# Second feed-forward of a macaron layer: the rests of its weights made by a negating cast on ScalarE and an accumulating transfer of the raw weights

## The chip, the cores and the metric

The kernel runs on one core of a Trainium2 chip. The metric is device time in microseconds (us), the median of several executions. One further execution was taken by the hardware profiler; its page and its trace are what the sections below read. PE is TensorE, DVE VectorE, ACT ScalarE, POOL GpSimd, SP SyncE.

## The reference: what is computed

One decoder layer on 512 tokens of 1024 features, all in float32: a SwiGLU feed-forward, a token mixing with eight heads, and a second SwiGLU feed-forward. Each is wrapped in two RMS norms and modulated by a condition vector.

```python
y = rmsnorm(h, ffn1_pre_g) * (1.0 + sc1) + sh1
y = swiglu(y, ffn1_w_gate, ffn1_w_up, ffn1_w_down)       # (silu(y @ w_gate) * (y @ w_up)) @ w_down, width 2816
h = h + 0.5 * g1 * rmsnorm(y, ffn1_post_g)
y = rmsnorm(h, mix_pre_g) * (1.0 + sc2) + sh2
y = token_mix(y, ...)                                    # ends in merged @ w_out
h = h + g2 * rmsnorm(y, mix_post_g)
y = rmsnorm(h, ffn2_pre_g) * (1.0 + sc3) + sh3
y = swiglu(y, ffn2_w_gate, ffn2_w_up, ffn2_w_down)
h = h + 0.5 * g3 * rmsnorm(y, ffn2_post_g)
```

## The kernel before, in words

**Products in three parts.** PE multiplies in the type float32r, which keeps fewer bits than float32. Every operand w is therefore kept as two float32r tiles: hi, which is w cast to float32r, and lo, the rest w - hi. `mm3` (lines 98 to 101) adds three products into PSUM: hi·hi (line 99), left hi · right lo (line 100), left lo · right hi (line 101). The product lo·lo is left out.

**A unit of weights.** Weights come in units of 128 partitions x 1024 float32, 512 KB each. `unit` (lines 83 to 96) loads one into a raw tile on the SP queue (line 88), casts it to hi on ACT (line 94), and subtracts on DVE (line 95):

```python
        nc.scalar.copy(hi, raw)
        nc.vector.tensor_tensor(out=lo, in0=raw, in1=hi.bitcast(F32), op=ALU.subtract)
```

The pools `wraw` and `wsp` hold four raw tiles, four hi tiles and four lo tiles, so unit u can be cast only when PE is done with the hi tile of unit u - 4. Each unit feeds 24 matmuls of 512 columns.

**Names.** A unit's name tells its stage: `a_f_g` and `b_f_g` are gate (g = 0) and up (g = 1) weights of the first and second feed-forward, `da_half_u` and `db_half_u` their down weights, `dm_half_u` those of w_out at the end of the token mixing, `ft`, `vh` and `mv` the other weights of the mixing. The hi and lo tiles of unit `db_1_0` are `h_db_1_0` and `l_db_1_0`; the profile leaves buffer numbers out and shows `h_db` and `l_db`. PSUM tiles are `pub` (up products of the second feed-forward), `pdm` and `pdb` (down products of the mixing and of the second feed-forward).

**The down products** (`down`, lines 223 to 268) go in two halves of 512 output features, each with four accumulators, one for 128 tokens. `db` has 11 units in a half. Units 0 to 6 are used as they come, 24 matmuls each. The last four units are held and used together, token tile by token tile: for i in 0 to 3, for u in 7 to 10, 6 matmuls. So the four hi tiles come free only at the end of a half, 6 matmuls apart, and the first four units of the next half take their place. `dm` has 4 units in a half: its first half uses them as they come, its second half holds all four.

**Second feed-forward** (`ffn2`): the first three up tiles f = 0, 1, 2 are computed for the first 256 tokens, then for the other 256, while the mixing's last two token tiles are still being normalised and transposed (`pst`). Tile f = 2 is split into space in `hT` (`dst` is given), the other tiles into the pool. From f = 3 on `up_tile` takes whole tiles, and one gate load `ada` goes with each until they are used up.

**Order.** The program is written with tile pools; a scheduler puts the instructions of each engine in order and adds the waits. Each engine runs its instructions in that order. POOL's instructions late in the program are the powers -1/2 of the norms (`rpm` and `rs`, lines 277 and 162) and some elementwise steps of the mixing (lines 574 and 590).

Of the kernel before, what the change touches and what calls it, by code (L numbers as in the profile page):

```python
# [17 lines left out]
D = 1024  # L18
# [10 lines left out]
def layer_kernel(ctx: ExitStack, tc: tile.TileContext, x, c, cols, gate_b,  # L29
# [21 lines left out]

# [1 line left out]
    h = resid.tile([P, NT, D], F32, name="h")  # L53
# [13 lines left out]

    # silu of the condition, a copy on every partition
    sg = small.tile([P, T], F32, tag="x2", name="sg")[0:2, :]
# [8 lines left out]

    # 1 + bias of the scales
    bs1 = const.tile([P, 24], F32, name="bs1")  # L80
    nc.gpsimd.tensor_scalar(bs1, col[:, 24:48], 1.0, None, ALU.add)

    def unit(src, n, name, dst=None, park=None):
        if park is None:
            raw = wraw.tile([P, 1040], F32, tag="raw", name=f"r_{name}")[:, :n]
        else:
            raw = wsp.tile([P, 1040], F32, tag=park, name=f"r_{name}")[:, :n]
        nc.sync.dma_start(raw, src)
        if dst is None:
            hi = wsp.tile([P, 1040], F32R, tag="hi", name=f"h_{name}")[:, :n]  # L90
            lo = wsp.tile([P, 1040], F32R, tag="lo", name=f"l_{name}")[:, :n]
        else:
            hi, lo = dst
        nc.scalar.copy(hi, raw)  # L94
        nc.vector.tensor_tensor(out=lo, in0=raw, in1=hi.bitcast(F32), op=ALU.subtract)  # L95
        return hi, lo
# [5 lines left out]

# [1 line left out]
    modc = [const.tile([P, 3, KT], F32, name=f"modc{s}") for s in range(3)]  # L104

    def ada(s, kind, j):
        """128 of the scales (0), shifts (1) or gates (2) of sub-layer s, features on partitions"""
        raw = wraw.tile([P, 1040], F32, tag="raw", name=f"a_{s}_{kind}_{j}")[:, :D]
        pieces = 2 if s + j == 0 and kind < 2 else 1
        for q in range(pieces):  # L110
            sl = slice(q * D // pieces, (q + 1) * D // pieces)
            nc.sync.dma_start(raw[:, sl], ada_w[(s * 3 + kind) * KT + j, :, sl])
        init = bs1[:, s * KT + j:s * KT + j + 1] if kind == 0 else col[:, 24 * (kind + 1) + s * KT + j:][:, 0:1]
        v = modc[s][:, kind, j:j + 1]
        parts = 4
        w = D // parts
        acc = v if parts == 1 else small.tile([P, 4], F32, tag="part", name=f"part{s}_{kind}_{j}")
        for q in range(parts):
            sl = slice(q * w, (q + 1) * w)
            nc.vector.tensor_tensor_reduce(out=raw[:, sl], in0=raw[:, sl], in1=sc[:, sl], scale=1.0,  # L120
                                           scalar=init if q == 0 else 0.0, op0=ALU.mult, op1=ALU.add,
                                           accum_out=acc[:, q:q + 1])
        if parts > 1:
            nc.vector.tensor_reduce(out=v, in_=acc[:, :parts], axis=AX.X, op=ALU.add)
# [7 lines left out]
    def gate_rows(s):  # L132
        """gate times post-norm gain, a row on every partition; sqrt(D) goes with the root of a sum in post"""
        g = modc[s][:, 2, :]
        nc.vector.tensor_tensor(out=g, in0=g, in1=col[:, 152 + s * KT:152 + (s + 1) * KT], op=ALU.mult)
        nc.vector.tensor_scalar(g, g, (1.0 if s == 1 else 0.5) * float(D) ** 0.5, None, ALU.mult)
        gates[s] = dram.tile([1, D], F32, name=f"gd{s}")
        nc.sync.dma_start(gates[s].rearrange("o (j p) -> p (o j)", p=P), g)
# [11 lines left out]
    def normed(i, s, halves=False):  # L150
        """the norm of token tile i of h, before its gain: two halves of the features"""
        if halves:
            n = [small.tile([P, T], F32, tag="ysb", name=f"n{s}_{i}_{q}", bufs=4) for q in range(2)]
            t = junk
        else:
            t = tmp_tile(f"n{s}_{i}")
            n = [t[:, :T], t[:, T:]]
        ss = small.tile([P, 1], F32, tag="ss", name=f"ss{s}_{i}", bufs=6)
        nc.scalar.activation(t, h[:, i, :], AF.Square, accum_out=ss)
        r = small.tile([P, NT], F32, tag="rstd", name=f"rs{s}_{i}", bufs=6)[:, :1]  # L160
        nc.vector.tensor_scalar(r, ss, 1.0 / D, EPS, ALU.mult, ALU.add)
        nc.gpsimd.tensor_tensor(out=r, in0=r, in1=mhalf[:, :1], op=ALU.pow)
        if not halves:
            nc.vector.tensor_scalar(t, h[:, i, :], r, None, ALU.mult)
            return n
        for q in range(2):
            nc.scalar.activation(n[q], h[:, i, q * T:(q + 1) * T], AF.Copy, scale=r)
        return n
# [7 lines left out]
    def y_token_tile(s, i, y, n):  # L176
        """n, the norm of token tile i of h, modulated, split and with features on partitions"""
        ts_ = slice(i * P, (i + 1) * P)
# [22 lines left out]

# [1 line left out]
    def swiglu_evac(f, psg, psu, hT, tag):  # L203
# [19 lines left out]
    def down(wd, hT, tag, s, nxt, n=NF, order=lambda f: f, pump=None, drain=None, rest=()):  # L223
        """h += gate * rmsnorm(hT.T @ wd); then, a token tile at a time, nxt = (sub-layer, y), the input of the next
        sub-layer, or the output. Returns what is still to be issued for the last two token tiles."""
        t0, ss0, later = [], [], []
# [57 lines left out]

# [1 line left out]
    def ffn1():  # L286
# [82 lines left out]

# [1 line left out]
    def mix(y, later):  # L371
        with ExitStack() as mc:
# [19 lines left out]

            # lower bound of the forget gates: first row of a softmax over two
            l0, l1 = col[:, 136:140], col[:, 140:144]
# [15 lines left out]

            # dependent chains of small products, issued between the parts of the projections
            chains = [[], []]
# [19 lines left out]

            # values of both groups, tokens on partitions
            vh = mp.tile([P, NT, T], F32, name="vh")
# [25 lines left out]

            # gates of the matrix memory: heads on partitions, time along the free dimension
            rowb = x2("rowb")[:NH, :]
# [43 lines left out]
            def merge(c, o, gate):  # L506
                """o: [token in tile, tile, channel] of a head, normalised; gate: [channel, token]"""
                pt = tr_tile(f"pmt{c}")
                for i in range(NT):
                    nc.tensor.transpose(pt[:, i * P:(i + 1) * P], o[:, i * P:(i + 1) * P], ident)  # L510
                t = x2s(f"mt{c}")
                nc.vector.scalar_tensor_tensor(out=t, in0=pt, scalar=col[:, 144 + c:145 + c], in1=gate,
                                               op0=ALU.mult, op1=ALU.mult)
                nc.scalar.copy(mhi[:, c, :], t)
                nc.vector.tensor_tensor(out=mlo[:, c, :], in0=t, in1=mhi[:, c, :].bitcast(F32), op=ALU.subtract)

            def transposed(name, k):
                """the first three blocks of 128 of k [channel, token], tokens on partitions: in PSUM, and a tile for it"""
                ps = tr_tile(f"pkt{name}")
# [5 lines left out]
            def states(S, pv, decay):  # L525
                """S[j] = decay[j] S[j - 1] + pv[j]"""
                nc.scalar.copy(S[:, 0, :], pv[:, 0, :])
# [3 lines left out]

            # the gated recurrence: channels on partitions
            def hgrn_head(hd):
# [31 lines left out]
                def raise_level(b, t):  # L565
                    """queries and keys from blocks of b to blocks of 2 b; t: products of the gates of blocks of b"""
                    n2 = T // (2 * b)
# [30 lines left out]
                def state():  # L598
                    """the state after each of the first three blocks of 128"""
                    ps = mm_tile(f"pu{hd}")  # L600
# [32 lines left out]

            # the matrix memory: causal convolution along the free dimension, silu; quadratic form
            def mlstm_head(hd):
# [23 lines left out]
                def weights():  # L659
                    """exponentials, arguments at most 0: rows s of the diagonal blocks; the queries' and the keys'  # L660
                    weights against the maximum at a block's end; the states' decays"""
                    E = s["E"] = mp.tile([P, 7 * P + 8], F32, tag="E", name=f"E{hd}", bufs=2)
# [118 lines left out]

# [1 line left out]
    def ffn2(y, later):  # L783
# [108 lines left out]
```

## Time and profile before

| | |
|---|---|
| three executions | 1060.78 us median, 1059.91 to 1061.39 |
| the profiled execution, first to last instruction (its own time is not listed apart) | 1058.7 us |
| PE busy | 1037.4 us, 98% of the span, clock granted 0.999 of full |
| DVE busy | 602.5 us, 57% |
| ACT busy | 344.6 us, 33% |
| POOL busy | 70.4 us, 7% |
| DMA | 136.39 MB, 129 GB/s on average |

The span is read first, then each engine's share of it; a busy PE close to the span says that other engines matter only where they make PE wait. Matmuls overlap: the profile gives one of 512 columns about 390 ns, while the next starts some 230 ns after it. The median lies 2.1 us above the profiled span; that is work before the first and after the last instruction, and run to run variation.

### The profile page before, as it was taken

To read this page: it belongs to the slowest core of one execution; us is meant where nothing else is said; L and a number is where in the kernel's file an instruction comes from. 1 tells how busy PE (TensorE), PEld (TensorE's weight loads), DVE (VectorE), ACT (ScalarE), POOL (GpSimd) and SP (SyncE) were. 2 spreads that over 40 slices of the span, in tenths; PEclk is the share of its full clock that TensorE was granted. 3 is DMA by queue.
4 is the path that set the end of the run, shared out by engine and by line. 5 is a ranking of instruction groups with operands and counts; after the bars stand their busy time and mean duration, and the time that the engine had idled before them with its cause. 6 is when DMAs were issued, how large, how long until landed. Compare 5 with 4: busy or idle time off the path is not lost.

```text
span 1058.7 us, 13118 instructions
## 1 busy us (share of the span) xinstructions
PE 1037.4 (98%) x4988; PEld 855.8 (81%) x4988; DVE 602.5 (57%) x1426; ACT 344.6 (33%) x496; POOL 70.4 (7%) x104
## 2 busy tenths in 40 slices
PE   6999999999999999999999999999999999999997
PEld 4788888888888878978888888898888888888886
DVE  7985465566555275388879775775543434322323
ACT  5542233222212164444343323632322222211311
POOL 1000000000000020021223140100000000000000
PEclk9999999999999999999999999999999999999999
DMA  9864444444555413333223311144353222222212
GB/s 339 278 219 144 155 144 159 159 159 167 191 179 162 151 61 128 108 122 111 100 80 102 98 61 60 56 148 148 126 138 121 99 85 96 100 100 80 100 40 80
DMA packets 42938, 136.39 MB, mean 129 GB/s; under 512 B 7670, under 2 KB 8054, under 8 KB 42876
## 3 DMA queue, kind: packets, MB, share of 16 engines
q1 hardware_dynamic: 42588, 135.41, 37.9%
q8 instruction: 39, 0.64, 0.2%
q10 hardware_dynamic: 288, 0.16, 0.1%
q14 instruction: 23, 0.19, 0.1%
HBM read 133.43 MB, written 2.12 MB: 128 GB/s over the span
## 4 chain that ended last, share of the span: by engine, by line
PE 84%; DVE 9%; DMA 2%; issue 2%; POOL 1%; ACT 1%; SPq 0%; DVEq 0%; POOLq 0%; ACTq 0%
PE pub L100 7%; PE pub L99 7%; PE pub L101 7%; PE pua L100 7%; PE pua L99 7%; PE pua L101 7%; PE pdb L99 4%; PE pdb L101 4%; PE pdb L100 4%; PE pda L99 4%; PE pda L101 4%; PE pda L100 4%; PE pft L99 3%; PE pft L100 3%; PE pft L101 3%; PE pl L561 2%
## 5 line engine op out<-in xcount | busy, mean ns | idle before, releaser
L100 PE MATMUL pub<-ylo,h_b 128*128 128x512 f32 (+1 forms) x368 | 137.6, 374 | 0.0
L99 PE MATMUL pub<-yhi,h_b 128*128 128x512 f32 (+1 forms) x368 | 137.6, 374 | 0.0
L101 PE MATMUL pub<-yhi,l_b 128*128 128x512 f32 (+1 forms) x368 | 137.1, 373 | 0.0
L100 PE MATMUL pua<-ylo,h_a 128*128 128x512 f32 x304 | 119.6, 394 | 0.0
L99 PE MATMUL pua<-yhi,h_a 128*128 128x512 f32 x304 | 119.5, 393 | 0.0
L101 PE MATMUL pua<-yhi,l_a 128*128 128x512 f32 x304 | 119.3, 392 | 0.0
L94 ACT CAST h_b<-r_b 128x1024 fp32r<-128x1024 f32 x42 | 44.0, 1050 | 140.1 <-issue 103.6
L95 DVE TENSOR_TENSOR l_b<-r_b,h_b 128x1024 fp32r<-128x1024 f32 x42 | 51.3, 1224 | 61.6 <-ACT h_b L94 61.6
L120 DVE CUSTOM_DVE_ANT_0 a<-a,sc 128x256 f32<-128x256 f32 x216 | 82.5, 426 | 0.0
L94 ACT CAST h_a<-r_a 128x1024 fp32r<-128x1024 f32 x38 | 39.9, 1050 | 125.4 <-issue 78.9
L99 PEld LDWEIGHTS pub<-yhi,h_b 128*128 128x128 f32 x368 | 69.2, 188 | 13.2
L100 PEld LDWEIGHTS pub<-ylo,h_b 128*128 128x128 f32 x368 | 69.3, 188 | 13.0 <-DVE ylo L199 0.2
L101 PEld LDWEIGHTS pub<-yhi,l_b 128*128 128x128 f32 x368 | 69.2, 188 | 13.0
L99 PE MATMUL pft<-yhi,h_ft 128*128 128x512 f32 x192 | 79.1, 412 | 0.0
L100 PE MATMUL pft<-ylo,h_ft 128*128 128x512 f32 x192 | 75.6, 394 | 0.0
L101 PE MATMUL pft<-yhi,l_ft 128*128 128x512 f32 x192 | 75.6, 394 | 0.0
L99 PE MATMUL pda<-h_da,hThi 128*128 128x512 f32 x176 | 69.5, 395 | 0.0
L99 PE MATMUL pdb<-h_db,hThi 128*128 128x512 f32 x176 | 69.3, 394 | 0.0
L101 PE MATMUL pda<-h_da,hTlo 128*128 128x512 f32 x176 | 69.2, 393 | 0.0
L101 PE MATMUL pdb<-h_db,hTlo 128*128 128x512 f32 x176 | 69.2, 393 | 0.0
L100 PE MATMUL pdb<-l_db,hThi 128*128 128x512 f32 x176 | 69.0, 392 | 0.0
L100 PE MATMUL pda<-l_da,hThi 128*128 128x512 f32 x176 | 69.0, 392 | 0.0
(270 smaller groups left out, 1936.7 us busy)
## 6 DMA issues: line engine op xcount, KB each, us to landing
a<-in_ada_w_dram SPq DMA_DIRECT2D x70, 512.0 KB, 4.0
r_b<-in_wgu_dram SPq DMA_DIRECT2D x44, 512.0 KB, 3.5
r_a<-in_wgu_dram SPq DMA_DIRECT2D x38, 512.0 KB, 3.9
r_ft<-in_w_ft_dram SPq DMA_DIRECT2D x24, 512.0 KB, 3.2
r_da<-in_wd_dram SPq DMA_DIRECT2D x22, 512.0 KB, 3.2
r_db<-in_wd_dram SPq DMA_DIRECT2D x22, 512.0 KB, 3.5
r_dm<-in_w_out_dram SPq DMA_DIRECT2D x8, 512.0 KB, 4.8
r_s<-in_wgu_dram SPq DMA_DIRECT2D x12, 256.0 KB, 6.7
```

Source lines behind the costliest of these rows:

```text
L94: nc.scalar.copy(hi, raw)
L95: nc.vector.tensor_tensor(out=lo, in0=raw, in1=hi.bitcast(F32), op=ALU.subtract)
L99: nc.tensor.matmul(ps, lhs[0], rhs[0], start=start, stop=False)
L100: nc.tensor.matmul(ps, lhs[0], rhs[1], start=False, stop=False)
L101: nc.tensor.matmul(ps, lhs[1], rhs[0], start=False, stop=stop)
L120: nc.vector.tensor_tensor_reduce(out=raw[:, sl], in0=raw[:, sl], in1=sc[:, sl], scale=1.0, scalar=init if q == 0 else 0.0, op0=ALU.mult, o ...
L561: nc.tensor.matmul(pv[:, i, :], kk[:, sl], qq[:, sl], start=True, stop=True)
```

## The change

For units of the stages `b`, `db` and `dm` that are split into the pool, the subtraction on DVE is gone. In its place ACT casts once more, hi to lo with the scale -1, and POOL issues a transfer that reads the raw weights again from DRAM and adds them to lo. What is left in lo is w - hi as before. Two units of `b` (tile f = 2, with `dst` given) and the stages `a`, `da`, `ft`, `vh` and `mv` keep the subtraction. Other lines of the diff take comments away and move line numbers by 4 behind line 95.

```diff
@@ -92,7 +92,11 @@
         else:
             hi, lo = dst
         nc.scalar.copy(hi, raw)
-        nc.vector.tensor_tensor(out=lo, in0=raw, in1=hi.bitcast(F32), op=ALU.subtract)
+        if dst is None and name[0] in "bd" and name[:2] != "da":
+            nc.scalar.activation(lo, hi.bitcast(F32), AF.Copy, scale=-1.0)
+            nc.gpsimd.dma_start(lo, src, accum_op=ALU.add)
+        else:
+            nc.vector.tensor_tensor(out=lo, in0=raw, in1=hi.bitcast(F32), op=ALU.subtract)
         return hi, lo
```

72 units take the new path: 42 of `b`, 22 of `db`, 8 of `dm`.

Three places show how the scheduler answers. The first is ACT where the second feed-forward's weights are first cast, at the end of the mixing; before, with `yf`, `n` and `yhi` belonging to the norm of the mixing's token tiles:

```order
L94 CAST h_b_0_5573<-r_b_0_5571 128x1024
L190 ACTIVATE yf_1_0_5512<-pst_1_0_5507,modc_108 128x128 x2
L159 ACTIVATE n_2_5494,ss_2_5495<-h 128x1024
L190 ACTIVATE yf_1_0_5512<-pst_1_0_5507,modc_108 128x128 x2
L198 CAST yhi_5090<-yf_1_1_5524 128x4x128
L94 CAST h_b_1_5579<-r_b_1_5577 128x1024
L94 CAST h_b_0_5585<-r_b_0_5583 128x1024
```

With the change, at the same place (line 96 is the negating cast):

```order
L94 CAST h_b_0_5581<-r_b_0_5579 128x1024
L194 ACTIVATE yf_1_0_5520<-pst_1_0_5515,modc_108 128x128 x4
L163 ACTIVATE n_2_5502,ss_2_5503<-h 128x1024
L96 ACTIVATE l_b_0_5582<-h_b_0_5581 128x1024
L94 CAST h_b_1_5588<-r_b_1_5586 128x1024
L202 CAST yhi_5090<-yf_1_1_5532 128x4x128
L278 ACTIVATE t1m_5558,ssbm_5557<-pdm_3_5336 128x512
L96 ACTIVATE l_b_1_5589<-h_b_1_5588 128x1024
L94 CAST h_b_0_5595<-r_b_0_5593 128x1024
L94 CAST h_b_1_5602<-r_b_1_5600 128x1024
L163 ACTIVATE n_3_5566,ss_3_5567<-h 128x1024
L96 ACTIVATE l_b_0_5596<-h_b_0_5595 128x1024
```

The negating cast of each unit stands behind other work of ACT, one to three instructions after the cast that it reads.

The second is PE at the boundary between the two halves of `db`, before:

```order
L99 MATMUL pdb_3_7328<-h_db_10_7559,hThi_5569 128x512
L100 MATMUL pdb_3_7328<-l_db_10_7560,hThi_5569 128x512
L101 MATMUL pdb_3_7328<-h_db_10_7559,hTlo_5570 128x512
L99 MATMUL pdb_0_7675<-h_db_0_7681,hThi_5569 128x512
L100 MATMUL pdb_0_7675<-l_db_0_7682,hThi_5569 128x512
```

With the change, at the same place:

```order
L103 MATMUL pdb_3_7378<-h_db_10_7619,hThi_5577 128x512
L104 MATMUL pdb_3_7378<-l_db_10_7620,hThi_5577 128x512
L105 MATMUL pdb_3_7378<-h_db_10_7619,hTlo_5578 128x512
L103 MATMUL pdb_0_7736<-h_db_0_7742,hThi_5577 128x512
L103 MATMUL pdb_1_7737<-h_db_0_7742,hThi_5577 128x512
L103 MATMUL pdb_2_7738<-h_db_0_7742,hThi_5577 128x512
L103 MATMUL pdb_3_7739<-h_db_0_7742,hThi_5577 128x512
L104 MATMUL pdb_0_7736<-l_db_0_7743,hThi_5577 128x512
```

The first product that reads the lo tile of the new half moves from second to fifth place. In the same way, the first product that reads the lo tile of a held last unit (`dm_1_3`, `db_0_10`, `db_1_10`) moves back: for `dm_1_3` behind 28 matmuls of its half's held part instead of 19, for the two of `db` behind 26 instead of 19.

The third is POOL at the end of the mixing, before:

```order
L277 TENSOR_TENSOR rpm_5488<-rpm_5488,mhalf 128x1
L162 TENSOR_TENSOR rs_2_5497<-rs_2_5497,mhalf 128x1
L277 TENSOR_TENSOR rpm_5552<-rpm_5552,mhalf 128x1
L162 TENSOR_TENSOR rs_3_5561<-rs_3_5561,mhalf 128x1
L277 TENSOR_TENSOR rpb_7940<-rpb_7940,mhalf 128x1
```

With the change, at the same place:

```order
L281 TENSOR_TENSOR rpm_5496<-rpm_5496,mhalf 128x1
L166 TENSOR_TENSOR rs_2_5505<-rs_2_5505,mhalf 128x1
L97 DMA l_b_0_5582<-in_wgu_dram 128x1024
L281 TENSOR_TENSOR rpm_5560<-rpm_5560,mhalf 128x1
L97 DMA l_b_1_5589<-in_wgu_dram 128x1024
L166 TENSOR_TENSOR rs_3_5569<-rs_3_5569,mhalf 128x1
L97 DMA l_b_0_5596<-in_wgu_dram 128x1024
```

The transfers now stand between the powers of the last two norms, and a power behind a transfer waits until that transfer has been issued.

## Rows read from the trace of the kernel before

**Rows 1.** The page's part 1: busy time, share and count of each engine.
```profile
span 1058.7 us, 13118 instructions
PE 1037.4 (98%) x4988; PEld 855.8 (81%) x4988; DVE 602.5 (57%) x1426; ACT 344.6 (33%) x496; POOL 70.4 (7%) x104
```
**Rows 2.** Stretches: PE, PEld, DVE, ACT, POOL busy (count), clock, DMA share, GB/s.
```profile
626.50:690.00 63.50, 61.05 (x330) 50.88 (x329) 42.95 (x86) 28.33 (x56) 10.78 (x14) 1.00 0.17 59
700.00:870.00 170.00, 170.00 (x821) 142.23 (x821) 79.20 (x148) 49.70 (x64) 0.00 (x0) 1.00 0.38 121
870.00:1040.00 170.00, 170.00 (x738) 138.25 (x737) 52.99 (x56) 40.37 (x52) 0.55 (x1) 1.00 0.23 83
905.00:910.00 5.00, 5.00 (x23) 4.05 (x22) 1.91 (x4) 1.57 (x2) 0.00 (x0) 1.00 0.28 105
```
**Rows 3.** Who PE waited for: total us, times, longest.
```profile
PE pl L561 <- DVE rm L726: 1.2, 1, 1.2
PE pmt L510 <- DVE oh L622: 0.8, 1, 0.8
PE pst L184 <- DVE n L164: 0.4, 1, 0.4
```
**Rows 4.** Groups: busy us, mean ns of one, idle before and releaser.
```profile
L94 ACT CAST h_b<-r_b 128x1024 fp32r<-128x1024 f32 x42 | 44.0, 1050 | 140.1 <-issue 103.6 <-PE pub L100 35.8 <-PE pdm L101 0.7
L95 DVE TENSOR_TENSOR l_b<-r_b,h_b 128x1024 fp32r<-128x1024 f32 x42 | 51.3, 1224 | 61.6 <-ACT h_b L94 61.6
L95 DVE TENSOR_TENSOR l_db<-r_db,h_db 128x1024 fp32r<-128x1024 f32 x22 | 27.0, 1226 | 68.7 <-ACT h_db L94 68.7
L95 DVE TENSOR_TENSOR l_dm<-r_dm,h_dm 128x1024 fp32r<-128x1024 f32 x8 | 9.8, 1224 | 9.1 <-ACT h_dm L94 9.1
```
**Rows 5.** Landing times of the 44 loads r_b, then of the 22 loads r_db.
```profile
DMA to landing us min/median/max: 3.3/3.5/10.8
...
DMA to landing us min/median/max: 3.4/3.5/4.8
```
**Rows 6.** Timeline of POOL: start, us, instruction, idle before.
```profile
677.41 0.55 POOL L277 TENSOR_TENSOR rpm<-rpm,mhalf 128x1 f32<-128x1 f32 x1 [2.33 <-DVE rpm L276]
690.53 1.40 POOL L162 TENSOR_TENSOR rs<-rs,mhalf 128x1 f32<-128x1 f32 x1 [3.93 <-DVE rs L161]
```
**Rows 7.** Timeline of ACT: casts of units that wait for a hi tile.
```profile
659.45 1.04 ACT L94 CAST h_dm<-r_dm 128x1024 fp32r<-128x1024 f32 x1
...
677.79 1.05 ACT L94 CAST h_b<-r_b 128x1024 fp32r<-128x1024 f32 x1 [0.71 <-PE pdm L101]
...
679.45 1.06 ACT L159 ACTIVATE n<-h 128x1024 f32<-128x1024 f32 x1
...
680.50 0.79 ACT L190 ACTIVATE yf<-pst,modc 128x128 f32<-128x128 f32 x2
...
963.84 1.05 ACT L94 CAST h_db<-r_db 128x1024 fp32r<-128x1024 f32 x1 [4.55 <-PE pdb L101]
969.41 1.05 ACT L94 CAST h_db<-r_db 128x1024 fp32r<-128x1024 f32 x1 [4.52 <-PE pdb L101]
...
987.46 1.05 ACT L94 CAST h_db<-r_db 128x1024 fp32r<-128x1024 f32 x1 [0.68 <-PE pdb L101]
...
1030.38 1.05 ACT L94 CAST h_db<-r_db 128x1024 fp32r<-128x1024 f32 x1 [4.55 <-PE pdb L101]
```
**Rows 8.** Timeline of PE: a held part's first matmul, first use of l_b, second half's first.
```profile
658.66 0.39 PE L99 MATMUL pdm<-h_dm,mhi 128*128 128x512 f32 x1
...
684.93 0.28 PE L101 MATMUL pub<-yhi,l_b 128*128 128x256 f32 x1
685.05 0.28 PE L99 MATMUL pub<-yhi,h_b 128*128 128x256 f32 x1
...
969.21 0.39 PE L99 MATMUL pdb<-h_db,hThi 128*128 128x512 f32 x1
...
991.46 0.39 PE L99 MATMUL pdb<-h_db,hThi 128*128 128x512 f32 x1
```

## The prediction

> **What bounds the kernel now.** I read the engines' shares first, then stretches, then PE's waits, then the timelines of ACT and PE at the places where weight tiles change hands. PE is busy 98% of a span of 1058.7 us, POOL 7% [rows 1]. By stretches PE has no gap from 700 to 1040 us; DVE is busy 47% and 31% of the two stretches there, ACT 29% and 24% [rows 2]. So in the second feed-forward the time is the number of matmuls, and DVE's subtraction is not what ends last. Only in the mixing's end, 626.5 to 690 us, is PE short of its stretch, by 63.50 - 61.05 = 2.45 us [rows 2], and there it waits for DVE: 1.2 + 0.8 + 0.4 us [rows 3]. That 2.4 us is all that a relieved DVE could give back.
>
> The pace: two casts of consecutive db units start 963.84 and 969.41 us, 5.57 us apart [rows 7]. A unit feeds 24 matmuls, so one matmul costs 0.232 us. Those of 256 columns start 0.12 us apart [rows 8].
>
> **What the change removes.** 72 subtractions on DVE: 42 x 1.224 + 22 x 1.226 + 8 x 1.224 = 88 us of DVE [rows 4]. Of these 64 (b and db) lie under PE's gapless stretch and are worth nothing while PE sets the pace; the 8 of dm and the first of b lie where PE waited 2.4 us for DVE in all. Which of those waits a subtraction caused the rows don't say; I count the gain as 0 and keep 2.4 us for the low end.
>
> **What it adds.** 72 casts on ACT of 128x1024. The negating form isn't in the trace; the nearest rows are the plain cast, 1.05 us, and another activation of the same shape, 1.06 us [rows 4, 7]. I take 1.05. ACT goes from 24% to under 45% of 870 to 1040 us: 31 or so casts more (5.57 us apart) are 32 us on top of 40. And 72 transfers on POOL, each of 512 KB, which read the weights a second time and also read lo back.
>
> **The unknown: I**, from the end of the negating cast to lo being whole. No transfer in the trace is issued by POOL and none accumulates. From below: the shortest plain load of the same size, 3.3 us from issue to landing; from above: the longest such load, 10.8 us, taken in a crowd of other loads [rows 5]. My value is built from rows near it: the plain median, 3.5 us [rows 5]; the bytes moved a second time, since lo has to be read too: 105 GB/s take a share of 0.28 of the DMA engines [rows 2], so 375 GB/s at a share of 1, and 512 KB takes 1.4 us; and POOL's own work for an issue, which I set near its small instructions, 0.55 to 1.40 us [rows 6], at 1.3. I = 3.5 + 1.4 + 1.3 = 6.2 us. The Trainium skill (DMA: Bandwidth & Descriptors, Anatomy of one DMA — SWDGE (gpsimd) path) fits a transfer issued from GpSimd, without accumulation, by 2.0 us + bytes/436 GB/s; as an estimate that is 3.2 us for 512 KB, the sum below would be near 5 us by it, and no run here shows it.
>
> **Where I is hidden.** In the running stages a unit's hi tile comes free three units before the unit is needed, 3 x 5.57 = 16.7 us. ACT's cast starts some 0.2 us later and takes 1.05, a sigmoid of a half PSUM tile may stand between (0.6), the negation takes 1.05: 13.8 us are left for I. So at 6.2, and even at 10.8, the running units of b and db cost nothing. Before, the same way took 1.05 + 1.23.
>
> **Where I shows.** At five places a tile comes free late. I count from the rows of before; each place moves all later ones with it.
>
> (1) Held part of dm. It begins at 658.66 [rows 8]; the last unit's cast starts at 659.45 [rows 7], the negation follows at once and ends near 661.5. In the new order 28 matmuls stand before the first use of that lo: 658.66 + 28 x 0.232 = 665.2. PE waits 661.5 + I - 665.2 = I - 3.7 = 2.5 us. What is queued behind the transfer on POOL (the power of the first norm) is only due after this part.
>
> (2) Start of b. The first cast starts at 677.79 [rows 7]. In the new order four small activations (0.4 each) and the square of n_2 (1.06) come first, and the negation ends near 682.65. PE first needs l_b at 684.93 [rows 8]: I - 2.3 = 3.9 us. The second unit's negation stands behind a cast, two more norm steps and ends near 686.1; the third ends near 690.2, the fourth 691.2. PE goes through a unit's half tile in 24 x 0.12 = 2.9 us, so the second unit costs another 0.9 and the third 1.2. Together I - 0.2 = 6.0 us. The last power, rs_3, stands behind the second transfer; the token tile that it serves is due after the first halves of three up tiles, over 10 us later, so I cost that at nothing; if those tiles ran out it would cost up to one issue, 1.3 us.
>
> (3) and (5) Held parts of db. The first begins at 969.21 [rows 8], its last unit's cast starts at 969.41 [rows 7] and the negation ends at 971.5. 26 matmuls stand before the use: 975.2. I - 3.7 = 2.5 us. The second half repeats this behind the cast at 1030.38 [rows 7]: 2.5 us.
>
> (4) Between the halves of db. The second half begins at 991.46 [rows 8]; four matmuls that need hi alone come first, so lo is due at 992.4. Its cast starts at 987.46 [rows 7], the negation ends at 989.55: I - 2.85 = 3.35 us. Four raw tiles come free in the same 5 us, and their loads run beside; the loads of db land in 3.5 us at the median and in 4.8 at most [rows 5], so I add 1.3. 4.65 us.
>
> **Sum**: 2.5 + 6.0 + 2.5 + 4.65 + 2.5 = 18.15, or 5 I - 12.85 us. At I = 10.8 it is 41.2; at I = 3.3 places 1, 3 and 5 vanish and 3.1 + 1.75 = 4.9 are left. The page gives the profiled execution's span alone, 1058.7, so the sum stands against that: 1076.9, and the median, 2.1 above the span, becomes 1060.8 + 18.1 = 1078.9.
>
> On POOL's work at place 2: DVE runs the scaling of n there, which reads and writes SBUF alone. The Trainium skill (SBUF — State Buffer, Who interferes with whom) says that such a copy, cast or tensor_scalar on DVE takes the port pair it shares with GpSimd for its whole length, and that descriptors are not written meanwhile; that speaks against issuing from POOL, and by it place 2 would grow by at most one such instruction. No row of this trace shows it, and the sum leaves it out.
>
> **The rivals.**
> - Covered: I near its lower end, under 4.5 us, so that one or two places show a few us. For it: the plain loads cluster at 3.5 us [rows 5]. Against: lo has to be read, and POOL has to issue. 1061 to 1070, of which the end within 0.2% needs I near 3.3 and DVE's 2.4 us returned.
> - Faster: DVE, 47% busy in the first stretch of the feed-forward and 68% in 626.5 to 690 [rows 2], leaves the mixing's end earlier and its waits go. Price 2.4 us [rows 3], so 1058.4. It decides only if lo is whole by the time the subtraction finished it, which at place 2 means I under 2.3 us; the shortest load of that size takes 3.3.
> - The DMA engines become the bound: accumulating may hold them far longer than moving the bytes twice. At a share of 0.38 for 700 to 870 us [rows 2] there is room for about 0.62 x 5.57 = 3.4 us of all engines for each unit. If one transfer held them for 6 us, a unit would take 1.4 + 6 = 7.4 instead of 5.57, and 64 units cost 64 x 1.8 = 117 us: 1178. Against: a plain unit needs 1.4 us, and this takes four times that.
> - That the change does something else: the order shows the 72 transfers and the 72 casts, so I give it no chance.
>
> **How the numbers follow.** What a measurement of this kernel can tell from no change is about 0.2%, 2.1 us. Stalls with I from 4.5 to 10.8 us: 75%. Covered: 11%, about half of it within 0.2%. Faster: 4%. DMA bound: 10%. The predicted time is that of the first case, 1078.9. The range goes from the covered case with DVE's gain, 1060.8 + 4.9 - 2.4 = 1063.3, to the upper bound, 1060.8 + 41.2 = 1102.0; the fast and the DMA bound cases, and the part of the covered one below it, are left out, under 20%. Slower by over 0.2%: 75 + 5 + 10 = 90%; within: 6%; faster: 4%.
>
> **What would show it.** Right: DVE near 515 us and ACT near 420 us busy; PE's matmul count unchanged and no gap from some 720 to 960 us; PE waits of a few us for POOL's transfers at five places, the longest at the start of b; landings of l_b near 5 us. Wrong: PE gaps at every unit of b or db (DMA engines or I over 13.8 us), no PE wait at the five places (I under 3.5 us), or matmuls that take longer each.

## The result, and the profile after

| | before | with the change |
|---|---|---|
| runs beside each other, median (us) | 1061.09 (1059.91 to 1061.43) | 1089.78 (1087.96 to 1090.62) |
| ratio, 95% interval | | 1.0272 (1.0259 to 1.0285) |
| span of the profiled execution (us) | 1058.7 | 1087.5 |
| PE busy, PE not busy (us) | 1037.4, 21.3 | 1046.6, 40.9 |

The change costs 28.7 us; 18.1 were forecast. The page's part 1 after the change, to be read beside [rows 1]:

```profile
span 1087.5 us, 13292 instructions
...
PE 1046.6 (96%) x4988; PEld 862.1 (79%) x4988; DVE 519.8 (48%) x1354; ACT 414.4 (38%) x568; POOL 130.3 (12%) x176
```

PE does the same 4988 matmuls. The span grew by 28.8 us, which splits in two: PE stands idle 19.6 us more, and its matmuls take 9.2 us longer. The idle part first. PE's waits (total us, times, longest) have three new lines among the first four, 18.7 us together:

```profile
PE pdb L104 <- DMA l_db<-in_wd_dram: 9.7, 3, 5.5
PE pub L105 <- DMA l_b<-in_wgu_dram: 6.7, 3, 5.4
...
PE pdm L104 <- DMA l_dm<-in_w_out_dram: 2.3, 1, 2.3
```

Where they are, in the timeline of PE (start, length, instruction, idle before and releaser):

```profile
668.17 0.63 PE L104 MATMUL pdm<-l_dm,mhi 128*128 128x512 f32 x1 [2.35 <-DMA l_dm<-in_w_out_dram]
...
694.97 0.58 PE L105 MATMUL pub<-yhi,l_b 128*128 128x256 f32 x1 [5.36 <-DMA l_b<-in_wgu_dram]
...
990.99 0.50 PE L104 MATMUL pdb<-l_db,hThi 128*128 128x512 f32 x1 [2.17 <-DMA l_db<-in_wd_dram]
...
1013.87 0.79 PE L104 MATMUL pdb<-l_db,hThi 128*128 128x512 f32 x1 [5.47 <-DMA l_db<-in_wd_dram]
...
1062.90 0.50 PE L104 MATMUL pdb<-l_db,hThi 128*128 128x512 f32 x1 [2.02 <-DMA l_db<-in_wd_dram]
```

These are the five forecast places, in their order: held part of dm, start of b, held part of db, boundary between db's halves, held part again. The negating casts that they wait for, in the timeline of ACT (beside [rows 7]; the second of these is the first unit of b):

```profile
661.04 1.06 ACT L96 ACTIVATE l_dm<-h_dm 128x1024 fp32r<-128x1024 f32 x1
...
686.06 1.06 ACT L96 ACTIVATE l_b<-h_b 128x1024 fp32r<-128x1024 f32 x1
...
983.71 1.06 ACT L96 ACTIVATE l_db<-h_db 128x1024 fp32r<-128x1024 f32 x1
...
1004.42 1.06 ACT L96 ACTIVATE l_db<-h_db 128x1024 fp32r<-128x1024 f32 x1
...
1055.87 1.06 ACT L96 ACTIVATE l_db<-h_db 128x1024 fp32r<-128x1024 f32 x1
```

From the end of each to the first matmul that reads the finished lo tile, the interval I of the prediction: 668.17 - 662.10 = 6.1, then 7.9, 6.2, 8.4 and 6.0 us. The three held parts lie at the 6.2 that was taken; the two places where many transfers run at once lie about 2 us above.

Now the longer matmuls. At the boundary between the halves, PE's timeline some matmuls after the wait and a little later:

```profile
1015.31 0.63 PE L104 MATMUL pdb<-l_db,hThi 128*128 128x512 f32 x1
1015.74 0.63 PE L105 MATMUL pdb<-h_db,hTlo 128*128 128x512 f32 x1
...
1020.22 0.39 PE L104 MATMUL pdb<-l_db,hThi 128*128 128x512 f32 x1
1020.45 0.40 PE L105 MATMUL pdb<-h_db,hTlo 128*128 128x512 f32 x1
```

They start 0.43 us apart up to 1019.6 us, and 0.23 apart behind it. The stretches (columns as in [rows 2]) show the granted clock there:

```profile
668.50:671.50 3.00, 3.00 (x8) 2.31 (x7) 0.23 (x2) 0.69 (x2) 0.00 (x0) 0.50 0.00 0
690.00:695.00 5.00, 0.03 (x1) 0.03 (x1) 2.62 (x5) 5.00 (x7) 2.06 (x4) 0.73 1.00 247
695.00:700.00 5.00, 5.00 (x27) 5.00 (x28) 3.83 (x7) 3.76 (x7) 1.71 (x2) 0.59 1.08 284
...
1010.00:1015.00 5.00, 1.13 (x3) 0.94 (x4) 0.00 (x0) 1.83 (x2) 1.72 (x2) 0.81 1.05 283
1015.00:1020.00 5.00, 5.00 (x14) 3.86 (x13) 0.00 (x0) 0.00 (x0) 0.00 (x0) 0.50 1.04 256
...
1064.50:1067.50 3.00, 3.00 (x9) 2.33 (x8) 2.22 (x4) 0.55 (x2) 0.56 (x1) 0.50 0.00 0
```

In the row from 1015 us PE is busy all 5 us with only 14 matmuls, at a clock of 0.50, which is 1.2 GHz instead of 2.4. In the clock record of the trace such half-clock stretches lie at four of the five places (3.4, 6.8, 6.8 and 3.4 us long, from about 668, 692, 1013 and 1064 us; none at the held part of 991 us); the record of before, which starts at 19 us, has none until 1056.4 us, 2.3 us before its end. PE works in 17.0 of these 20.4 us, the rest lies in the waits, and loses half of them: 8.5 of the 9.2 us. The first and the last row show the half clock with no DMA traffic at all, a share of 0.00; so traffic during the matmuls is not what slows them there.

At the other two places the DMA engines are full, a share of 1.00 to 1.08, and there lo comes later. In the DMA records the first packet of a transfer leaves 1.6 us after the start of its issue at the held part of dm, and lo is used 4.0 us behind that. At the boundary of db the first packet leaves after 1.6 us too, but 6.4 us follow. At the start of b it leaves only after 3.05 us, and 4.4 follow. That the full engines make the transfers slow is the likely reading, since no run takes the other loads away; why the first packet leaves late at the start of b is open.

Away from these places PE waits for no transfer of lo. The long stretches, beside [rows 2] (the first begins inside the start of b, whose later units cost PE its missing 1.4 us; the second holds two of the places):

```profile
700.00:870.00 170.00, 168.63 (x861) 142.89 (x860) 48.34 (x130) 75.03 (x92) 24.38 (x28) 1.00 0.86 210
870.00:1040.00 170.00, 162.36 (x689) 131.05 (x688) 17.25 (x25) 68.58 (x80) 24.35 (x28) 0.98 0.77 176
```

DVE's load in them fell from 79.20 to 48.34 and from 52.99 to 17.25 us, worth nothing; the DMA share rose from 0.38 to 0.86 and from 0.23 to 0.77.

### The profile page after: what moved, and what is told of

It is laid out like the page before. It is cut to its first block, busy times and chain, and to the rows that moved or that the text cites. A ratio compares the mean times of both kernels' runs of the same rounds, so it can differ in the third digit from the quotient of the medians.

```text
span 1087.5 us, 13292 instructions
## 1 busy us (share of the span) xinstructions
PE 1046.6 (96%) x4988; PEld 862.1 (79%) x4988; DVE 519.8 (48%) x1354; ACT 414.4 (38%) x568; POOL 130.3 (12%) x176
## 5 line engine op out<-in xcount | busy, mean ns | idle before, releaser
L104 PE MATMUL pdb<-l_db,hThi 128*128 128x512 f32 x176 | 71.5, 406 | 9.7 <-DMA l_db<-in_wd_dram 9.7
L103 PEld LDWEIGHTS pua<-yhi,h_a 128*128 128x128 f32 x304 | 57.1, 188 | 13.2
```

Of the source, the lines that this page charges most:

```text
L103: nc.tensor.matmul(ps, lhs[0], rhs[0], start=start, stop=False)
L104: nc.tensor.matmul(ps, lhs[0], rhs[1], start=False, stop=False)
```

## The experiments

The theory, T: the loss is PE standing still at the five places, because lo comes some 6 us after the negating cast of a unit whose hi tile came free late, and PE's clock falls behind such a wait. The rivals: R1, doubled traffic or POOL's issues cost a little at every unit; R2, it is the transfers, not PE's standing still, that slow the matmuls.

**The streaming units alone, and the late units alone.** Two kernels, which split the 72 units at the five places:

```diff
-        if dst is None and name[0] in "bd" and name[:2] != "da":
+        part = name.split("_")
+        late = (name[:4] == "dm_1" or (name[0] == "b" and int(part[1]) < FF2_F)
+                or (name[:2] == "db" and (part[2] in ("9", "10") or (part[1] == "1" and part[2] in ("0", "1")))))
+        if dst is None and name[0] in "bd" and name[:2] != "da" and not late:
```

The second kernel has `and late` at the end of the last line.

Expected of the 58 streaming units:

> The new path for the 58 units that stream only; the 14 units whose hi tile comes free late (dm_1_0 to 3, the first four of b, db_0_9, db_0_10, db_1_0, db_1_1, db_1_9, db_1_10) keep the subtraction on DVE. Theory T (the loss is PE's stalls at the five hand-over places, 18.7 us of waits for l tiles, and the half clock that follows each stall, 9.2 us; streaming units are hidden): 1061 us, within 3 us of the kernel before, no PE wait for a transfer of l_b or l_db, clock 1.00 throughout. Rival R1 (the doubled DMA traffic or POOL's issues cost a little at every unit): 58/72 of the loss of 28.7 us stays, 1084 us. Rival R2 (matmuls are slowed by the DMA traffic itself): PE's busy time stays near 1046 us.

Measured: 1061.68 us against 1061.15 for before, ratio 1.0010 (1.0001 to 1.0019). Its page and its stretch of 700 to 960 us:

```profile
span 1059.7 us, 13278 instructions
...
PE 1037.4 (98%) x4988; PEld 856.1 (81%) x4988; DVE 535.3 (51%) x1368; ACT 401.3 (38%) x554; POOL 119.7 (11%) x162
```

```profile
700.00:960.00 260.00, 260.00 (x1213) 215.67 (x1213) 58.61 (x138) 117.78 (x139) 40.05 (x46) 1.00 0.89 204
```

PE has no gap at a DMA share of 0.89, and no wait for a transfer of lo; its clock is 0.999 of full, as before. R1 falls. DVE's 67 us less bring nothing either.

Expected of the 14 late units:

> The converse: the new path for the 14 late units only, 58 streaming units keep the subtraction. T: the same five waits and the same falls of the clock, 1085 to 1090 us. R1: 14/72 of the loss, 1066 to 1067 us. If the crowd of transfers makes the late ones slow, a middle value: landings nearer 5.3 than 6.2 us and the sum of the waits some 4 us shorter, 1083 us.

Measured: 1089.09 us, ratio 1.0257 (1.0240 to 1.0274): a loss of 27.9 us, nearly the whole, from 14 of 72 units, with the same waits.

```profile
PE pdb L107 <- DMA l_db<-in_wd_dram: 9.7, 3, 5.7
PE pub L108 <- DMA l_b<-in_wgu_dram: 7.2, 3, 4.9
...
PE pdm L107 <- DMA l_dm<-in_w_out_dram: 2.4, 1, 2.4
```

So the other 58 transfers add little or nothing: 0.7 us lie between the medians of the two kernels, within their intervals. PE is busy 1045.9 us here; the half clock lies at the last four places and, 3.4 us long, at 456 us in the mixing, which is none of the five.

**A standstill without transfers.** The clock's part needed a test with no transfer by POOL in the program: the kernel before, with the subtraction of the unit that opens db's second half repeated on DVE.

```diff
-        nc.vector.tensor_tensor(out=lo, in0=raw, in1=hi.bitcast(F32), op=ALU.subtract)
+        for _ in range(8 if name == "db_1_0" else 1): nc.vector.tensor_tensor(out=lo, in0=raw, in1=hi.bitcast(F32), op=ALU.subtract)
```

> The kernel before, without any transfer by POOL: the subtraction of the unit that opens the second half of db is done eight times over on DVE (same result), so that its lo is ready 7 x 1.226 = 8.6 us later. PE stands still there for about 5.9 us (lo at 998.3 us instead of 989.7, needed at 992.4). T with a clock that falls because PE stood still: 5.9 us and behind it a stretch of 3.4 to 6.8 us at half clock, which costs half its length: 1068.7 to 1070.4 us in all, PE's busy time 1039 to 1041. R2 (the clock falls, or matmuls lengthen, because of the DMA traffic of the accumulating transfers): 5.9 us alone, 1067 us, clock 1.00 throughout, PE busy 1037.4.

The same edit with 5 and with 4 in place of 8:

> As the run with eight subtractions, with five: lo of the unit that opens the second half of db is ready after seven subtractions and one product of 0.68 us from 989.4 us, at 998.3, and PE stands still for 4.9 us without any transfer by POOL, about as long as at that place in the full change. T (the clock falls because PE stands still): a stretch of half clock behind it, 6.8 us at most, PE's busy time 1039 to 1041, 1067.5 to 1070 us. R2 (the clock falls because of accumulating transfers): 4.9 us alone, 1066 us, PE busy 1037.4.

> The same with four subtractions: a stall of 2.5 us, as at the held parts in the full change. In the runs so far stalls of 2.0 to 2.4 us were followed by half clock in some places and not in others (none at the first place when that was the only one). T: 2.5 to 4.2 us, 1063.5 to 1065.3 us. R2: 2.5 us, 1063.5 us.

Measured:

| subtractions | wait at that place | loss, median (interval) |
|---|---|---|
| 8 | 9.6 us | 12.1 (10.6 to 13.6) |
| 5 | 4.8 us | 7.1 (5.8 to 8.5) |
| 4 | 2.6 us | 3.9 (2.9 to 5.5) |

The waits in PE's list (total us, times, longest), in the same order:

```profile
PE pdb L100 <- DVE l_db L95: 9.6, 1, 9.6
...
PE pdb L100 <- DVE l_db L95: 4.8, 1, 4.8
...
PE pdb L100 <- DVE l_db L95: 2.6, 1, 2.6
```

The first wait was longer than the 5.9 us expected, because the scheduler put three other units' subtractions between the repeated ones, and so that kernel came out above T's range; the other two lie in theirs. Each loss is above its wait, and the interval leaves the wait alone out. PE's timeline in the kernel with five:

```profile
997.87 0.68 PE L100 MATMUL pdb<-l_db,hThi 128*128 128x512 f32 x1 [4.82 <-DVE l_db L95]
998.34 0.63 PE L101 MATMUL pdb<-h_db,hTlo 128*128 128x512 f32 x1
998.77 0.63 PE L99 MATMUL pdb<-h_db,hThi 128*128 128x512 f32 x1
...
1002.31 0.39 PE L99 MATMUL pdb<-h_db,hThi 128*128 128x512 f32 x1
1002.54 0.39 PE L100 MATMUL pdb<-l_db,hThi 128*128 128x512 f32 x1
```

The same 0.43 us between starts behind a wait for DVE, then 0.23. The granted clock is 0.50 from 998 to 1001 us and 1.00 from 1002 us on. The half clock lasts 10.2, 3.4 and 3.4 us in the three kernels; of the first the wait itself still covers about half. So R2 falls for the clock: PE standing still is enough, with no transfer by POOL in the program. The sizes are rough. In the kernel with five, another half-clock stretch of 3.4 us lies at 455 us, in the mixing, and PE's 2.4 us of longer matmuls are shared between the two; there the timeline speaks for T, and the interval not by itself.

**One place alone.** The new path for the second half of dm only:

```diff
-        if dst is None and name[0] in "bd" and name[:2] != "da":
+        if name[:4] == "dm_1":
```

> The new path for the four units of the second half of dm only, so that of the five places only the first is left. T: one PE wait of 2.3 us on l_dm and one stretch of 3.4 us at half clock behind it, 2.3 + 1.7 = 4.0 us: 1065 us. If the stalls of the full change had partly replaced other waits of PE in the mixing: 1062 to 1063 us. R1: 4/72 of 28.7, 1062.7 us.

Measured: 1065.88 us, ratio 1.0047 (1.0035 to 1.0060), a loss of 4.8 us. The wait on `l_dm` is there, 2.4 us, but no half clock follows it (granted clock 1.00 from 665 to 675 us, PE busy 1037.8 us); in its place 0.8 us of waiting for DVE's `l_b` at the start of b and smaller waits appeared. The total was forecast for a reason that only half holds: a wait of some 2 us is followed by half clock in some places and not in others.

**Filling the standstill.** The full change, with idle PE given work:

```diff
+                if tag == "b" and half == 1 and u == 0:
+                    for i in range(NT):
+                        for _ in range(5):
+                            nc.tensor.matmul(acc[i], hT[0][:, 0, i * P:(i + 1) * P], v[0][:, 0, :], start=True, stop=True)
...
+                    if hf + f == 0:
+                        for _ in range(40):
+                            nc.tensor.matmul(ps[0][0][:, sl], us[0][0][0][:, 0, :], y[0][:, 0, sl], start=True, stop=True)
```

> The full change, and PE is given work in two of the stalls: 40 matmuls of 256 columns ahead of the first product of b and 20 of 512 columns ahead of the second half of db, each of which starts its accumulation anew, so that the real products overwrite them. They cost PE about 40 x 0.12 = 4.8 us and 20 x 0.232 = 4.6 us, in time in which it waited 5.4 and 5.5 us. T (the clock falls because PE stands still): the waits at these two places shrink to about 1 us, the two stretches of half clock behind them (6.8 us each, which cost 3.4 us each) are gone, about 1083 us, PE's busy time without the extra matmuls about 1040. R2 (the clock falls, or the matmuls are slow, whatever PE did before): no gain, 1089 us or, if the extra work comes in front instead of in the gap, up to 1098 us.

Measured: 1089.84 us, ratio 1.0263 (1.0247 to 1.0280), no gain, where T had forecast 1083 us: a miss, and by its total the figure of R2. By its parts it is not R2's. The waits on l_b and l_db fell from 16.4 to 10.3 us and the two long half-clock stretches from 6.8 to 3.4 us each, which gives back half of that, 3.4 us; but the extra matmuls took 9.4 us, and the waits did not shrink to 1 us but to some 3: -6.1 - 3.4 + 9.4 is nothing gained. Shorter standstills, shorter half clock; filling them with work that nobody needs pays nothing here. Behind the wait of 2.2 us on `l_dm` there is no half clock in this run either.

**The price of accumulating.** POOL's transfer plain:

```diff
-            nc.gpsimd.dma_start(lo, src, accum_op=ALU.add)
+            nc.gpsimd.dma_start(lo, src)
```

> The full change with POOL's transfer plain instead of accumulating: lo then holds the raw weights instead of the rest, with the same bytes written. It prices the accumulation. T: the landing falls from 5.3 at least to some 3.5 to 4.5 us and the waits at the five places by 1 to 1.8 us each, 5 to 9 us in all, with some of the low clock gone: 1075 to 1084 us; the DMA engines' time for one transfer falls from 3.07 to about 1.5 us. If accumulating is free and POOL's issue is the price: same landing, 1089 us.

Measured: 1076.6 us, ratio 1.0148 (1.0132 to 1.0163), in T's range. The waits on lo fell from 18.7 to 11.4 us and the half clock from 20.4 to 10.2. The queues (packets, MB, share of 16 engines' span; q0 is POOL's) with the change, then with plain transfers:

```profile
q1 hardware_dynamic: 42588, 135.41, 36.3%
q0 software_dynamic: 10368, 37.75, 20.3%
```

```profile
q1 hardware_dynamic: 42588, 135.41, 39.3%
q0 software_dynamic: 10368, 37.75, 12.8%
```

The transfers of `l_b`, issue (ns, min/median/max) and landing (us from the start of the issue), in the same order:

```profile
L97 POOL DMA_DIRECT2D l_b<-in_wgu_dram x42: 862/872/894, 687.5 to 924.4; - x42
...
DMA to landing us min/median/max: 5.3/6.2/11.8
```

```profile
L97 POOL DMA_DIRECT2D l_b<-in_wgu_dram x42: 527/528/742, 685.9 to 918.8; - x42
...
DMA to landing us min/median/max: 3.7/4.3/12.6
```

An accumulating transfer of 512 KB holds all 16 DMA engines for 0.203 x 1087.5 / 72 = 3.07 us, a plain one for 0.128 x 1076.7 / 72 = 1.91, where 1.5 had been expected. The accumulating one lands 1.9 us later at the median, POOL issues it in 0.87 us instead of 0.53, and 13 of the 28.7 us hang on it. The Trainium skill (Collectives: The Full Stack, The bandwidth ceiling: the fold count and why AG ≠ RS ≠ AR) says of the add in a reduce-scatter that it is slow because it reads two sources, not by the adding, and that this halves the rate; here the engines' time grew by a factor of 1.6.

**More tiles.** The full change with five hi and lo tiles, and the kernel before with the same as a control:

```diff
-    wraw = ctx.enter_context(tc.tile_pool(name="wraw", bufs=4))
-    wsp = ctx.enter_context(tc.tile_pool(name="wsp", bufs=4))
+    wraw = ctx.enter_context(tc.tile_pool(name="wraw", bufs=3))
+    wsp = ctx.enter_context(tc.tile_pool(name="wsp", bufs=5))
```

> The full change with five hi and five lo tiles and three raw tiles in place of four of each: at every hand-over one unit finds its tile a unit (5.57 us) earlier. T (what costs is that lo comes 6 us after a tile that comes free late): the waits at the held parts of dm and db and between the halves of db vanish, a few us at most are left at the start of b, where ACT's queue delays the negation; no fall of the clock without a stall: 1061 to 1066 us. Rival (the price of the transfer itself, wherever it is issued): 1085 to 1090 us.

> The kernel before with the same buffers, five hi, five lo, three raw: the control of the run above. Its lo was never late, so all theories expect 1061 us within 2; three raw tiles could cost something where loads are slow (the first feed-forward starts with 10.8-us landings), up to 5 us more, and that much would then have to be taken off the run above.

Measured: 1071.30 and 1066.06 us, beside 1061.06 for before. The other sizes cost 5.0 us by themselves (of it 2.2 us are PE's longer idle time from 450 to 500 us, in the mixing); with these taken off, the full change lies at 1066.3, just above T's range, and adds 5.2 instead of 28.7 us. The 10.8-us landing, which the control's expectation puts at the first feed-forward, is one of `r_b`; the loads `r_a` there take 8.4 at most. The waits of the full change:

```profile
PE pub L105 <- DMA l_b<-in_wgu_dram: 3.6, 1, 3.6
...
PE pdb L104 <- DMA l_db<-in_wd_dram: 0.4, 1, 0.4
```

The places in dm and db are gone, as T has it. The start of b stays, since there ACT's queue delays the negation: the cast ends at 681.87, the negation starts at 684.72. Behind this wait of 3.6 us the half clock lasts 6.8 us. Neither kernel beats the one before.

**The idea where DVE is busiest.** Two attempts to be faster than both kernels, with the new path for the units of `ft` alone, then without the first four:

```diff
+    fts = []
...
-        if dst is None and name[0] in "bd" and name[:2] != "da":
+        fts.append(name) if name[:2] == "ft" else None
+        if name[:2] == "ft" and len(fts) > 4:
```

The first kernel has `if name[:2] == "ft":` in place of the last line, and no list.

> The idea of the change put where DVE is busiest: the kernel before, with the new path for the 24 units of ft (mixing), where DVE was busy 80 to 88% from 450 to 600 us, and nowhere else. It is meant to beat both kernels. For it: 24 x 1.22 = 29 us of DVE go, and PE waited some 4 us for DVE in the mixing; if they go, 1057 to 1060 us. Against: ACT takes 25 us more, POOL's elementwise steps of the mixing stand in its queue behind the transfers, and a hi tile of ft that comes free late shows a lo 6 us late, 2 to 6 us at each such place: 1063 to 1080 us. The second is the likelier, since units of ft are cast as PE frees their tiles.

> As the run with the new path for the 24 units of ft, but the first four of them, whose hi tiles come free late behind the value weights, keep the subtraction; the other 20 take the new path. T: the wait of 5.5 us on l_ft, the one of 1.5 us on h_ft and the half clock behind them are gone, so 1061 to 1063 us; if 24 us less of DVE's work also shortens PE's waits for DVE in the mixing (some 4 us in all in the kernel before), 1058 to 1060 us, faster than both kernels. Rival (ACT's and POOL's queues in the mixing cost as well): 1064 to 1068 us.

Measured: 1071.55 us (ratio 1.0102, 1.0087 to 1.0118) and 1065.64 us (1.0041, 1.0028 to 1.0055). In the first, a tile that comes free late showed again, 5.5 us on `l_ft` with 6.8 us of half clock there. In the second that is gone and the clock is full, but the time is the rival's: PE's wait for DVE's `qq` in the mixing grew from 0.2 to 3.4 us, though DVE had less to do. What does that is open.

## Why the prediction was right, and where its size was off

- **What bounds, and DVE's gain of 0**: right. 83 us fewer on DVE (602.5 to 519.8) bought nothing; the run of the streaming units shows it alone.
- **Running units hidden**: right, by the same run.
- **The five stalls**: right in place, order and size. Forecast 2.5, 6.0, 2.5, 4.65, 2.5, together 18.15 us; measured 2.3, 6.7, 2.2, 5.5, 2.0, together 18.7. The run of the 14 late units shows that they carry nearly the whole loss. That the sums lie so close is partly luck: the held parts came out below their forecast, the two other places above it. At the start of b the first unit cost 5.4 instead of 3.9 us, the later ones 1.4 instead of 2.1. The longest single wait was at the boundary of db, 5.5 us, and not at the start of b, which has the larger sum; and `l_b` landed in 6.2 us at the median, not near 5.
- **I = 6.2**: right at the held parts (6.0 to 6.2), too short where transfers crowd (7.9 and 8.4, against 6.2 and, with the 1.3 added, 7.5). What it is made of: a landing of 5.7 us at the median for `l_dm`, issue included, and some 0.4 us from the negation to the issue. Its terms were off on either side: POOL's issue takes 0.87 us where 1.3 was put in, and accumulating adds 1.9 us to the landing where the second reading was put at 1.4; that they still add up to 6.2 is partly luck. The Trainium skill (DMA: Bandwidth & Descriptors, Anatomy of one DMA — SWDGE (gpsimd) path) has a fit for a transfer from GpSimd that gives, as an estimate, 3.2 us for 512 KB; beside it stand 3.7 at least and 4.3 at the median in the run with plain transfers, so it is a little low here, and it doesn't price the accumulation.
- **The step that failed is the sum's form**: it took the stalls as the whole cost, 5 I - 12.85, with every matmul at its old pace. A stall here costs itself and, behind it, matmuls at 1.2 GHz. The longer matmuls are 9.2 us in the profile, nearly all of the difference between 18.1 and 28.7. The prediction named longer matmuls as a sign that it was wrong, but gave them no price. The Trainium skill (TensorE: Matmul & The Clock Gate, HAM oscillation — how this bites in real kernels) tells of a kernel in which PE waits for a DMA in each turn of its loop and comes back throttled each time; the trace agrees at four of the five places, 0.43 us between matmuls against 0.23.
- **DMA engines the bound**: wrong, but nearer than its chance said. 3.4 us of all engines were free for a unit, and the transfer took 3.07; the share reached 0.86 from 700 to 870 us, and the engines were full at two of the five places.
- **DVE blocking POOL at place 2**: not seen. The issues there took 0.89 us, those of `l_b` 0.87 at the median. The late first packet there, 3.05 us after the start of the issue, is not explained by it either: in the kernel with the 14 late units alone the issue stands beside the same DVE instruction, and the first packet leaves after 1.6 us.

## What to carry to other kernels

Price a longer way to an operand at the few places where its buffer comes free late, not per use: 14 of 72 units carried 27.9 of the 28.7 us, and relieving an engine that nothing waits for bought nothing. Where PE runs without a gap, price a stall at more than itself: here half as much again came behind it as half-clock matmuls. Measure an accumulating transfer's landing, its issue and its time on the DMA engines before building on it: here each is well above that of the same transfer without the addition.

## What was unexpected of the hardware

- Waits of 3 to 10 us in a program at full clock were followed by 3.4 to 10.2 us at 1.2 GHz (part of which the wait itself still covers); waits of 2.0 to 2.6 us by 3.4 us or by none. At one spot of the mixing a wait of 1.0 to 1.3 us was followed by 3.4 us in two kernels (five subtractions, 14 late units) and by none in the kernel before. What decides between these is open.
- Half clock does not need DMA traffic: two of the four stretches had a DMA share of 0.00.
- An accumulating DMA of 512 KB: 5.3 us at least from issue to landing, 3.07 us of all 16 engines, 0.87 us of POOL; the same transfer plain: 3.7, 1.91 and 0.53.
